# One-core hybrid encoder layer with mixture of experts: single-pass gather, third-largest expert at 64 rows, two more modulation blocks on VectorE, splits 3 to 1 by GpSimd

## The chip, the cores and the metric

The kernel runs on one core of a Trainium2 chip. The metric is device time in microseconds for one execution, the median of the runs of a kernel. Its engines are TensorE (PE, with the weight load shown apart as PEld), VectorE (DVE, `V` in the code), ScalarE (ACT, `S`), GpSimd (POOL, `G`) and SyncE (SP, whose queue issues nearly all transfers). The work of each engine runs in the order in which the program lists it.

## The reference

One encoder layer on 256 positions of width 2048, in fp32. `c` gives six modulation rows of 2048 each (shift, scale and gate of the mixer, sections 0 to 2; the same of the expert part, sections 3 to 5):

```python
c_act = silu(c)
mod = c_act @ w_ada + b_ada                  # 2048 x 12288
sh1, sc1, g1, sh2, sc2, g2 = split(mod, 6)
h = rms_norm(x, g_mix) * (1 + sc1) + sh1
z = h @ w_in                                 # 2048 x 4616
y = concat[gmlp(z), pool(z), forgetting_attention(z)]
x = x + g1 * (y @ w_out)
h = rms_norm(x, g_ffn) * (1 + sc2) + sh2
scores = sigmoid(h @ w_router)               # 16 experts, 4 groups
# best group of each position, its best 2 experts, weights normalised
x = x + g2 * sum over the 2 experts of weight * (silu(h @ w_gate[e]) * (h @ w_up[e])) @ w_down[e]
```

The 16 experts have matrices 2048 x 1024, 2048 x 1024 and 1024 x 2048. Each of the 256 positions goes to two of them, so 512 assignments are spread over the experts.

## The kernel before

**Dense part.** Weights come through ring tiles of 1 MiB (`ring`, `spare`, later `ringm`), issued on SP's queue. A product that must be accurate is made of three fp32r products (`mm3`): `split` writes the high part of a 128x512 weight tile by a ScalarE cast and the low part by a subtraction on VectorE or GpSimd, as a letter of `WSPLIT` (w_in) or `WSO` (w_out) says. Four letters stand for the four 128-row tiles of one piece (512 x 512 weights). `step` runs the preparation of tiles four ahead of their products. w_in is gone through in five chunks of rows (`CHUNKS`, 2, 2, 4, 4 and 4 tiles of 128); for each, `make_h` brings the normalised, modulated columns of x into the form `hT`, and nine pieces are multiplied and added into `z` (`put`). `PLAN` and `LAST` list by hand what goes between the pieces of a chunk: modulation steps (`n`, `m`, `0`, `1`), attention steps (`a`), norms (`w`).

A modulation block (512 columns of a section) is `c_act @ w_ada` for four ring tiles. `ada_parts` makes it on TensorE, as 16 products with a one-column operand into four rows of a PSUM bank (32 rows in the trace, two for each); `sum_parts` makes it on VectorE, as 16 multiply-adds over 128x512 (L292, L294), the last of which leaves PSUM (`ga`). The letters of `M1A`, `M1B`, `M2A`, `M2B` and `G1` say which. Both kinds use the two banks `accs`. The gate rows (sections 2 and 5) get their bias by one more product with `bgt`.

w_out is four column blocks of four pieces. A block's two PSUM banks are multiplied by the gate and added to x by `x1_block`; the banks come from a pool of three (`pm`).

**Handover.** The router's logits come from x (`logit_a`, `logit_b`). Then one long VectorE chain picks groups and experts (`oh1`, `oh2`, `M`), counts (TensorE products into `pp`), orders the experts by their count (`key`, `ohc`, `po`), and writes the expert numbers to `irow`, which SP reads to know which weights to load. It goes on to the slot of each assignment and to one-hot matrices `oneh` (128 x 512 for each half of x). The remaining gate blocks of section 5 run on TensorE in between (`g2_run`). `gather` multiplies x (fp32) by `oneh`: 512 slots of tokens, sorted by expert, in `XT`. Slots 0 to 255 are gathered before the banks are handed over, slots 256 to 511 after it; `oneh` lies in the last ring tile.

**Expert part.** Experts are taken by rank of their count; `CAPS` gives each rank its number of rows (128, 64 or 32), `ORDER` the order of the ranks, and the last rank is left out. An expert is twelve tiles of 2 MiB in six ring tiles (`wide`): eight for gate and up, four for down. At 128 rows the weights are split in the same way and multiplied three times (`el`); at 64 and 32 rows the fp32 weights are used. If a rank has more tokens than rows, a loop at the end takes that expert once more (`n_ov`).

## Time and profile before

| | |
|---|---|
| median of 3 runs | 1436.28 us (1435.34 to 1439.57) |
| the profiled execution | 1442.07 us, its span 1440.2 us |
| mean granted TensorE clock | 0.962 |
| busy: TensorE, VectorE, ScalarE, GpSimd | 87%, 48%, 29%, 11% of the span |
| moved | 539 MB, 374 GB/s over the span |

The span is what lies between the first and the last instruction of the profiled execution; times in the rows count from its start. Weights alone are 535.85 MB read. The dense part ends at about 476 us with the router's logits, the expert part begins at 532 us.

### The profile page before, as it was taken

Reading aid. Unit: us, or ns where it says so; the run is one execution under the profiler, and the core shown is the slowest. Engines: PE = TensorE matmul, PEld = TensorE weight load, DVE = VectorE, ACT = ScalarE, POOL = GpSimd, SP = SyncE. Lnnn points to the kernel's source line nnn. Section 1 sums busy time; section 2 is a strip of 40 time slices with the busy share of each in tenths; the row PEclk is TensorE's granted clock in tenths of the full one; section 3 lists DMA queues with packets and bytes.
Section 4 is the critical chain, followed back from the end, with each engine's and each line's share of the span. In section 5 each row is a group of like instructions: output and inputs, shape, how many; then the busy total and the mean of one; then the engine's idle time right before and its main releaser. Section 6 shows DMA issues by size and latency. Waiting matters only on the chain.

```text
span 1440.2 us, 17629 instructions
## 1 busy us (share of the span) xinstructions
PE 1247.2 (87%) x6844; PEld 683.4 (47%) x6844; DVE 693.2 (48%) x1271; ACT 417.1 (29%) x754; POOL 160.5 (11%) x127
## 2 busy tenths in 40 slices
PE   5998999998999896999969999689997889858876
PEld 3665776664776372764326743257533222222221
DVE  4466675755795643893228842269611211202112
ACT  4532334445343140771006820048300000000000
POOL 1333332312443000000000000000000000000000
PEclk9999999999999898999989999899999999989988
DMA  9979696889888579998999989999899999999997
GB/s 391 377 312 348 237 375 227 313 334 352 355 301 344 212 296 428 427 415 339 427 426 426 424 315 428 428 425 427 308 420 426 425 427 427 426 427 426 427 427 296
DMA packets 49209, 539.15 MB, mean 374 GB/s; under 512 B 5464, under 2 KB 5592, under 8 KB 7008
## 3 DMA queue, kind: packets, MB, share of 16 engines
q1 hardware_dynamic: 47664, 534.79, 90.7%
q10 hardware_dynamic: 1456, 3.17, 0.6%
q8 instruction: 55, 0.90, 0.3%
q14 instruction: 34, 0.28, 0.1%
HBM read 535.85 MB, written 2.10 MB: 374 GB/s over the span
## 4 chain that ended last, share of the span: by engine, by line
PE 59%; DMA 26%; DVE 7%; issue 3%; ACT 2%; POOL 1%; SPq 0%; DVEq 0%; ACTq 0%; POOLq 0%
PE lbank L171 29%; PE pm L171 18%; DMA ring<-in_e_down_dram 11%; DMA ringl<-in_e_gu_dram 7%; DMA ring<-in_e_gu_dram 7%; PE bank L171 6%; PE ada L171 4%; PE pt L171 1%; DVE ada L294 1%; DMA ring<-in_w_ada_dram 1%; DVE whl L176 1%; DVE el L176 1%; ACT whl L175 1%; DVE z L451 1%; POOL whl L176 0%
## 5 line engine op out<-in xcount | busy, mean ns | idle before, releaser
L171 PE MATMUL pm<-whl,hT 128*128 128x512 f32 x1120 | 296.6, 400 | 9.7 <-DVE whl L176 3.9
L171 PEld LDWEIGHTS pm<-whl,hT 128*128 128x128 f32 x1120 | 208.8, 190 | 82.9 <-issue 12.8
L171 PE MATMUL lbank<-ringl,xr 128*32 128x256 f32 (+1 forms) x1152 | 143.1, 494 | 38.1 <-DMA ringl<-in_e_gu_dram 37.8
L171 PE MATMUL lbank<-el,xs 128*128 128x512 f32 x576 | 138.3, 398 | 9.5 <-ACT el L175 6.5
L176 POOL TENSOR_TENSOR whl<-ring,whl 128x512 fp32r<-128x512 f32 x86 | 120.0, 1407 | 225.4 <-ACT whl L175 201.9
L171 PE MATMUL lbank<-ring,xr 128*32 128x256 f32 (+1 forms) x864 | 104.3, 484 | 34.8 <-DMA ring<-in_e_gu_dram 34.7
L171 PEld LDWEIGHTS lbank<-el,xs 128*128 128x128 f32 x576 | 108.1, 190 | 39.9 <-ACT el L175 9.7
L175 ACT CAST whl<-ring 128x512 fp32r<-128x512 f32 x172 | 99.9, 622 | 72.6 <-PE pm L171 62.5
L171 PE MATMUL bank<-y,gt 128*128 128x512 f32 x240 | 118.0, 614 | 0.0
L1304 DVE TENSOR_TENSOR xa<-xa,bank 128x512 f32<-128x512 f32 x120 | 82.5, 688 | 68.5 <-PE bank L171 68.5
L171 PE MATMUL lbank<-ring,hidT 128*64 128x512 f32 (+1 forms) x576 | 104.6, 630 | 10.9 <-DMA ring<-in_e_down_dram 10.9
L171 PEld LDWEIGHTS lbank<-ringl,xr 128*32 128x32 f32 (+1 forms) x1152 | 52.0, 127 | 129.1 <-issue 68.0
L1295 DVE TENSOR_TENSOR y<-lbank,g2w 128x512 f32<-128x512 f32 x60 | 41.5, 692 | 147.9 <-PE lbank L171 147.9
L176 DVE TENSOR_TENSOR whl<-ring,whl 128x512 fp32r<-128x512 f32 x86 | 83.9, 991 | 38.0 <-ACT whl L175 37.7
L175 ACT CAST el<-ring 128x512 fp32r<-128x512 f32 x144 | 90.0, 625 | 29.3 <-PE lbank L171 21.6
L176 DVE TENSOR_TENSOR el<-ring,el 128x512 fp32r<-128x512 f32 x144 | 92.7, 689 | 0.0
L1191 ACT COPY gt<-bank 128x256 f32<-128x256 f32 x15 | 5.6, 373 | 290.0 <-PE bank L1189 290.0
L1245 DVE TENSOR_TENSOR hid<-hid,lbank 128x512 f32<-128x512 f32 x12 | 8.3, 688 | 164.7 <-PE lbank L171 164.5
L171 PEld LDWEIGHTS lbank<-ring,xr 128*32 128x32 f32 (+1 forms) x864 | 39.1, 127 | 98.8 <-DMA ring<-in_e_gu_dram 48.9
L171 PE MATMUL ada<-ring,cact 128*1 128x512 f32 (+1 forms) x568 | 68.6, 585 | 19.7 <-DMA ring<-in_w_ada_dram 14.0
L171 PE MATMUL lbank<-el,hidT 128*128 128x512 f32 x288 | 74.9, 412 | 12.1 <-DVE el L176 8.3
L175 ACT CAST el<-ringl 128x512 fp32r<-128x512 f32 x96 | 58.7, 624 | 79.5 <-DMA ringl<-in_e_gu_dram 64.8
(377 smaller groups left out, 1185.4 us busy)
## 6 DMA issues: line engine op xcount, KB each, us to landing
ringl<-in_e_gu_dram SPq DMA_DIRECT2D x60, 2048.0 KB, 20.1
ring<-in_e_gu_dram SPq DMA_DIRECT2D x45, 2048.0 KB, 24.3
ring<-in_e_down_dram SPq DMA_DIRECT2D x45, 2048.0 KB, 25.7
ring<-in_w_ada_dram SPq DMA_DIRECT2D x79, 1024.0 KB, 7.1
ring<-in_w_in_dram SPq DMA_DIRECT2D x30, 1024.0 KB, 8.2
ringm<-in_e_gu_dram SPq DMA_DIRECT2D x15, 2048.0 KB, 21.0
ringm<-in_e_down_dram SPq DMA_DIRECT2D x15, 2048.0 KB, 21.5
ring<-in_w_out_dram SPq DMA_DIRECT2D x12, 1024.0 KB, 8.2
```

Source lines behind the costliest of these rows:

```text
L171: E.matmul(out, lhsT=lhsT, rhs=rhs, start=start, stop=stop, skip_group_check=True)
L175: S.copy(hi, src)
L176: (eng or V).tensor_tensor(lo, src, hi.bitcast(F32), op=OP.subtract)
L294: eng.scalar_tensor_tensor(P, w[:, j, :], ck, P, op0=OP.mult, op1=OP.add)
L451: V.tensor_tensor(dst, dst, P[h], op=OP.add)
L1191: S.copy(gt, p[:, :256])
L1245: V.tensor_tensor(hid[:, o], hid[:, o], P[2 * b + 1], op=OP.mult)
L1295: V.tensor_tensor(y, P, g2w[:, c0:c0 + 512], op=OP.mult)
L1304: V.tensor_tensor(a, a, p, op=OP.add)
```

## The change

- `CAPS`: the third rank has 64 rows instead of 128.
- `M2A` "VVPP": the first two blocks of section 3 move from TensorE to VectorE, so seven modulation blocks are there. `WSPLIT` and `WSO`: in the last three chunks and in w_out three of four tiles are split by GpSimd.
- `make_h`: x is scaled by ScalarE (`scaled`) and transposed, instead of multiplied by a diagonal matrix.
- The three `pm` banks are fixed tiles; from w_out on the second modulation bank joins them as the fourth, and all gate blocks use the first one.
- Gate biases: eight row transfers on ScalarE's queue (`bgr`) and an add on VectorE (`gate_row`, L797), instead of a product with `bgt`.
- The gather uses x in two fp32r parts (`x_hi` on ScalarE, `x_lo` on VectorE, L1004) for all 512 slots at once, before the banks are handed over. The operands lie where the last two ring tiles (`ringl`) lie afterwards; the older ring tiles are loaded first.

```diff
-CAPS = [128] * 3 + [64] * 6 + [32] * 6 + [0]
+CAPS = [128] * 2 + [64] * 7 + [32] * 6 + [0]
-M1A, M1B, M2A, M2B, G1 = "PPVV", "PPPP", "PPPP", "PPPP", "PVVV"
-WSPLIT, WSO = ["VGVG"] * 5, "VGVG"
+M1A, M1B, M2A, M2B, G1 = "PPVV", "PPPP", "VVPP", "PPPP", "PVVV"
+WSPLIT, WSO = ["VGVG", "VGVG", "GVGG", "GVGG", "GVGG"], "GVGG"
...
-    psM, s_psM = pool("psM", 3, space=PSUM)
+    psM, s_psM = pool("psM", 1, space=PSUM)
+    pbanks = deque(psM.tile([128, 512], F32, name=f"pm{i}") for i in range(3))
+
     def pm():
-        return psM.tile([128, 512], F32, name="pm")
+        pbanks.rotate(-1)
+        return pbanks[-1]
...
-                if g == ng - 1 and bias is not None:
-                    mm(P[0:1, :], ident[0:8, bias:bias + 1], bgt, start=False)
...
+    def scaled(q):
+        k0, nk = CHUNKS[q]
+        for h in range(2):
+            S.activation(xn[:, h, :128 * nk], xa[:, h, 128 * k0:128 * k0 + 128 * nk], AF.Identity, scale=rsx[:, h:h + 1])
...
-                mm(p[:, 128 * h:128 * h + 128], xa[:, h, 128 * k:128 * k + 128], diag[:, h, :])
+                E.transpose(p[:, 128 * h:128 * h + 128], xn[:, h, 128 * c:128 * c + 128], ident)
...
+    def gate_row(sec, q, out, P):
+        S.copy(out, P)
+        o = slice(32 * q, 32 * q + 1)
+        V.tensor_tensor(out[o, :], out[o, :], bgr[o, sec // 3, :], op=OP.add)
+
     def gate_args(sec, q, out):
-        return sec, 4 * q, 4, lambda P: S.copy(out, P), q % 2, 4 * (sec // 3) + q
+        return sec, 4 * q, 4, lambda P: gate_row(sec, q, out, P), 0
...
+    bgr = rt.tile([128, 2, 512], F32, name="bgr")
+    for q in range(4):
+        for a in range(2):
+            nc.scalar.dma_start(bgr[32 * q:32 * q + 1, a, :], bg_d[a:a + 1, 512 * q:512 * q + 512])
...
+    g1_load(1)
+    pbanks.append(accs[1])
...
+    def x_hi():
+        for c, h in parts:
+            o = slice(1024 * c, 1024 * c + 1024)
+            S.activation(xhl[:, 0, h, o], xa[:, h, o], AF.Identity, scale=rs1[:, h:h + 1])
+
+    def x_lo(n):
+        for _ in range(n):
+            c, h = parts.pop(0)
+            o = slice(1024 * c, 1024 * c + 1024)
+            V.scalar_tensor_tensor(xhl[:, 1, h, o], xa[:, h, o], rs1[:, h:h + 1], xhl[:, 0, h, o].bitcast(F32),
+                                   op0=OP.mult, op1=OP.subtract)
...
     V.reciprocal(sc, sc)
+    x_hi()
...
+    x_lo(2)
...
     V.tensor_copy(irow[:, 0:16], po[0:1, 0:16])
+    x_lo(2)
...
-    def gather(half, k, bank):
-        o = slice(256 * half, 256 * half + 256)
-        p = bank()
+    def gather(k):
+        p = pm()
         for h in range(2):
-            mm(p[:, :256], xa[:, h, 128 * k:128 * k + 128], oneh[:, h, o], start=h == 0, stop=h == 1)
+            for i in range(2):
+                mm(p, xhl[:, i, h, 128 * k:128 * k + 128], oneh[:, h, :], h + i == 0, h + i == 2)
...
+    s_phl.close()
+    pl, s_pl = pool("pl", 1, side="right")
+    wides += [pl.tile([128, 2 * RINGW], F32, name=f"ringl{i}") for i in range(RING_LAST)]
+    wide_ring = deque([t for _, t in sorted(zip(used, old), key=lambda x: x[0])] + wides[RING + RING_MORE:])
...
-    for k in range(KD):
-        gather(1, k, bank)
```

Where instructions come to stand. First VectorE's queue in the handover, from `M` (both experts of each position) to `irow` (the expert numbers); `grow` are the gate rows, `xhl` the two parts of x. Before:

```order
L1001 TENSOR_TENSOR M<-oh_3680,oh_3687 128x32
L1029 SCALAR_TENSOR_TENSOR key<-pt_119,rev 128x16
L1030 SCALAR_TENSOR_TENSOR keyc<-pt_119,revc 16x1
L1032 TENSOR_SCALAR rkc<-key,keyc 16x16
L1033 TENSOR_REDUCE rkc<-rkc 16x1
L1035 TENSOR_SCALAR ohc<-ioE,rkc 16x16
L1041 CAST irow<-pt_120 1x16
```

Now:

```order
L1050 TENSOR_TENSOR M<-oh_3602,oh_3609 128x32
L797 TENSOR_TENSOR grow_3322<-grow_3322,bgr 1x512
L797 TENSOR_TENSOR grow_3323<-grow_3323,bgr 1x512
L1004 SCALAR_TENSOR_TENSOR xhl<-xa,rs_3524,xhl 128x1024 x2
L1079 SCALAR_TENSOR_TENSOR key<-pt_122,rev 128x16
L1080 SCALAR_TENSOR_TENSOR keyc<-pt_122,revc 16x1
L1082 TENSOR_SCALAR rkc<-key,keyc 16x16
L1083 TENSOR_REDUCE rkc<-rkc 16x1
L1085 TENSOR_SCALAR ohc<-ioE,rkc 16x16
L797 TENSOR_TENSOR grow_3324<-grow_3324,bgr 1x512
L1091 CAST irow<-pt_123 1x16
```

Two bias adds and two low parts have come ahead of `key`, and the bias add of the last gate block ahead of `irow`.

Next SP's queue from the last gate tiles to the loads of the first expert (`ring_63`, `ring_64`, `ring_65`, `ringm` are the older ring tiles, `ringl` the last two). Before:

```order
L147 DMA ring_64<-in_w_ada_dram 128x2048
L1316 TENSOR_LOAD irow
L1312 ISA
L1312 DMA ringl_3792<-in_e_gu_dram 128x4096
L1312 ISA
L1312 DMA ringl_3793<-in_e_gu_dram 128x4096
L1312 ISA
L1312 DMA ringm_2773<-in_e_gu_dram 128x4096
```

Now:

```order
L147 DMA ring_64<-in_w_ada_dram 128x2048
L1356 TENSOR_LOAD irow
L1352 ISA
L1352 DMA ringm_2671<-in_e_gu_dram 128x4096
L1352 ISA
L1352 DMA ring_65<-in_e_gu_dram 128x4096
L1352 ISA
L1352 DMA ring_63<-in_e_gu_dram 128x4096
```

The four older tiles come first, the two `ringl` tiles behind them.

Last VectorE's queue in the last chunk, from the norm factors of the first heads (`hr`) on; `z<-z,hr` are the norms, `z<-z,pm` the puts, `ada` the sums of a modulation block, `whl` the splits. Before:

```order
L352 TENSOR_TENSOR hr_1893<-hr_1893,hr1t 128x16
L176 TENSOR_TENSOR whl<-ring_64,whl 128x512
L451 TENSOR_TENSOR z<-z,pm 128x512 x2
L176 TENSOR_TENSOR whl<-ring_64,whl 128x512
L569 TENSOR_TENSOR z<-z,hr_1893 128x512 x2
L451 TENSOR_TENSOR z<-z,pm 128x512 x2
L176 TENSOR_TENSOR whl<-ring_63,whl 128x512
L584 TENSOR_SCALAR qk<-pt_120,prm_69 128x256
L558 TENSOR_REDUCE ss_2008<-pt_119 128x4
L558 TENSOR_REDUCE ss_2008<-ada_113 128x4
L176 TENSOR_TENSOR whl<-ring_63,whl 128x512
```

Now:

```order
L292 TENSOR_SCALAR ada_114<-ring_63,cact 128x512
L294 SCALAR_TENSOR_TENSOR ada_114<-ring_63,cact,ada_114 128x512 x3
L573 TENSOR_TENSOR z<-z,hr_1825 128x512 x2
L454 TENSOR_TENSOR z<-z,pm_119 128x512
L454 TENSOR_TENSOR z<-z,pm_120 128x512
L294 SCALAR_TENSOR_TENSOR ada_114<-ring_64,cact,ada_114 128x512 x4
L588 TENSOR_SCALAR qk<-pt_123,prm_69 128x256
L562 TENSOR_REDUCE ss_1936<-pt_122 128x4
L562 TENSOR_REDUCE ss_1936<-ada_113 128x4
L294 SCALAR_TENSOR_TENSOR ada_114<-ring_65,cact,ada_114 128x512 x4
L176 TENSOR_TENSOR whl<-ring_63,whl 128x512
```

Three times four multiply-adds have come in, and two of the splits have gone.

## Rows read from the trace of the kernel before

**Rows 1.** The page, part 2: the span in 40 slices of 36 us, GB/s moved in each.

```profile
GB/s 391 377 312 348 237 375 227 313 334 352 355 301 344 212 296 428 427 415 339 427 426 426 424 315 428 428 425 427 308 420 426 425 427 427 426 427 426 427 427 296
```

**Rows 2.** Two stretches of the dense part: start and end, length, then busy time (instructions) of PE, PEld, DVE, ACT and POOL, granted clock, share of the transfer engines, GB/s. The first is the last chunk of w_in, the second w_out.

```profile
226.00:358.00 132.00, 125.67 (x750) 79.17 (x749) 82.11 (x194) 63.66 (x141) 31.39 (x27) 1.00 0.83 312
358.00:471.00 113.00, 106.13 (x509) 78.97 (x508) 81.95 (x103) 44.64 (x85) 48.05 (x38) 0.97 0.86 334
```

**Rows 3.** The same columns for stretches of the handover and of the expert part.

```profile
488.00:496.00 8.00, 6.97 (x52) 2.53 (x50) 4.70 (x20) 0.59 (x1) 0.00 (x0) 1.00 0.00 0
496.00:520.00 24.00, 21.85 (x84) 16.70 (x83) 18.60 (x61) 12.35 (x22) 0.00 (x0) 0.93 0.95 389
520.00:532.00 12.00, 12.00 (x55) 9.10 (x53) 3.81 (x7) 3.62 (x7) 0.00 (x0) 1.00 0.23 98
...
646.00:676.00 30.00, 29.08 (x120) 13.69 (x120) 12.83 (x22) 6.37 (x11) 0.00 (x0) 1.00 0.82 310
676.00:826.00 150.00, 129.38 (x733) 71.23 (x730) 79.82 (x133) 53.06 (x89) 0.00 (x0) 0.94 1.01 426
826.00:868.00 42.00, 40.16 (x165) 19.30 (x165) 18.03 (x30) 9.79 (x17) 0.00 (x0) 1.00 0.86 329
868.00:1006.00 138.00, 118.28 (x679) 64.07 (x674) 72.94 (x122) 46.86 (x79) 0.00 (x0) 0.94 1.01 427
1006.00:1054.00 48.00, 45.23 (x185) 24.18 (x185) 24.91 (x41) 16.08 (x27) 0.00 (x0) 1.00 0.86 331
1054.00:1420.00 366.00, 287.34 (x1746) 97.69 (x1742) 65.47 (x123) 5.79 (x13) 0.00 (x0) 0.95 1.01 427
```

**Rows 4.** The page, part 5: the matmuls of the three experts with 128 rows, gate and up first, then down (count; busy us, mean ns; idle before).

```profile
L171 PE MATMUL lbank<-el,xs 128*128 128x512 f32 x576 | 138.3, 398 | 9.5 <-ACT el L175 6.5
...
L171 PE MATMUL lbank<-el,hidT 128*128 128x512 f32 x288 | 74.9, 412 | 12.1 <-DVE el L176 8.3
```

**Rows 5.** The waits of SP's queue from 486 to 500 us (total us, times, longest).

```profile
SPq L1316 <- DVE pos L1045: 11.2, 1, 11.2
SPq L1312 <- PE ada L171: 3.6, 1, 3.6
```

**Rows 6.** The timeline of SP's queue: start, us, issue, count.

```profile
496.39 0.89 SPq L1312 DMA_DIRECT2D ringl<-in_e_gu_dram  x2
...
532.22 0.33 SPq L1312 DMA_DIRECT2D ring<-in_e_gu_dram  x1
```

**Rows 7.** The chain that ended last, the piece of the second half of the gather: start, us, engine, name, line, count.

```profile
517.89 14.31 PE bank L171 x64
```

**Rows 8.** Groups of instructions from 0 to 480 us, shapes apart: TensorE's modulation blocks, VectorE's sums, GpSimd's splits, and two ScalarE operations over 512 and 2048 columns.

```profile
L176 POOL TENSOR_TENSOR whl<-ring,whl 128x512 fp32r<-128x512 f32 x86 | 120.0, 1407 | 225.4 <-ACT whl L175 201.9 <-PE ada L171 15.5 <-issue 8.0
L175 ACT CAST whl<-ring 128x512 fp32r<-128x512 f32 x172 | 99.9, 622 | 72.6 <-PE pm L171 62.5 <-DMA ring<-in_w_in_dram 4.2 <-DVE z L451 2.7
...
L171 PE MATMUL ada<-ring,cact 128*1 128x512 f32 x408 | 51.7, 596 | 5.6 <-DVE ga L297 4.4 <-ACT r L311 1.2
...
L294 DVE SCALAR_TENSOR_TENSOR ada<-ring,cact,ada 128x512 f32<-128x512 f32 x54 | 40.7, 754 | 1.5
...
L375 ACT ACTIVATE hT<-xa 128x2048 fp32r<-128x2048 f32 x2 | 3.8, 1902 | 0.3 <-DMA xa<-in_x_dram 0.3
```

**Rows 9.** The split's line L176: duration in ns, shortest/median/longest, first and last start, shape.

```profile
L176 DVE TENSOR_TENSOR whl<-ring,whl x86: 677/693/1803, 25.4 to 450.2; 128x512 fp32r<-128x512 f32 x86
L176 POOL TENSOR_TENSOR whl<-ring,whl x86: 1257/1296/1798, 26.0 to 451.7; 128x512 fp32r<-128x512 f32 x86
```

**Rows 10.** The timeline of the dense part: start, us, engine, line, out<-in, count, in brackets the idle time before and what ended it.

```profile
127.04 1.04 PE L171 MATMUL ada<-ring,cact 128*1 128x512 f32 x8 [4.41 <-DVE ga L297]
...
253.28 1.38 DVE L451 TENSOR_TENSOR z<-z,pm 128x512 f32<-128x512 f32 x2
...
267.20 5.78 PE L171 MATMUL pm<-whl,hT 128*128 128x512 f32 x24
```

**Rows 11.** TensorE's waits from 360 to 476 us (total us, times, longest).

```profile
PE pm L171 <- DVE xg L855: 3.7, 3, 1.8
```

**Rows 12.** The timeline of the handover: the Exp of the scores, the gate blocks of TensorE (`ada`), VectorE's `key`, `irow` and first one-hot (it lies in `ring`).

```profile
478.76 0.23 ACT L969 ACTIVATE sc<-sc 128x32 f32<-128x32 f32 x1 [2.25 <-DVE sc L968]
482.35 3.59 PE L171 MATMUL ada<-ring,cact 128*1 128x512 f32 x16
485.71 2.21 PE L171 MATMUL ada<-ringm,cact 128*1 128x512 f32 x16
490.40 0.17 DVE L1029 SCALAR_TENSOR_TENSOR key<-pt,rev 128x16 f32<-128x16 f32 x1 [5.61 <-PE pt L171]
491.71 3.61 PE L171 MATMUL ada<-ring,cact 128*1 128x512 f32 x32
491.82 0.16 DVE L1041 CAST irow<-pt 1x16 int32<-1x16 f32 x1 [0.48 <-PE pt L171]
495.70 0.54 DVE L1085 TENSOR_SCALAR ring<-io,sl,rs 128x512 f32<-128x512 f32 x1
```

**Rows 13.** Three stretches of the handover, columns as in rows 2; the granted clock is the third number from the end.

```profile
480.00:486.00 6.00, 6.00 (x26) 0.78 (x26) 4.08 (x24) 0.59 (x1) 0.00 (x0) 0.50 0.88 330
...
500.00:504.00 4.00, 4.00 (x13) 3.21 (x12) 3.66 (x15) 1.56 (x3) 0.00 (x0) 0.57 1.01 428
504.00:532.00 28.00, 28.00 (x121) 21.50 (x119) 14.89 (x46) 13.69 (x24) 0.00 (x0) 1.00 0.68 287
```

More of the change, by code (lines that the diff above doesn't have):

```diff
@@ L253, in ada_load, with ada_parts @@
         return w.rearrange("p (k n) -> p k n", n=n)
-    def ada_parts(sec, k0, nk, after, acc, bias=None):
+    def ada_parts(sec, k0, nk, after, acc):
         P = accs[acc]
@@ L266, in run @@
                     k, t = r * g + j, j % 4
-                    mm(P[32 * t:32 * t + 1, :128 * nk], cact[:, k:k + 1], w[:, j, :], start=k < 4,
-                       stop=k >= KD - 4 and (t > 0 or bias is None))
-                if g == ng - 1 and bias is not None:
-                    mm(P[0:1, :], ident[0:8, bias:bias + 1], bgt, start=False)
+                    mm(P[32 * t:32 * t + 1, :128 * nk], cact[:, k:k + 1], w[:, j, :], start=k < 4, stop=k >= KD - 4)
                 if g == ng - 1:
@@ L377, in body @@
     rsqrt(rsx, ssx, D, [128, 2], "rx")
-    diag = pa.tile([128, 2, 128], F32, name="diag")
-    for h in range(2):
-        V.tensor_scalar(diag[:, h, :], ident, rsx[:, h:h + 1], None, op0=OP.mult)
     jc = pa.tile([128, 16], F32, name="jc")
@@ L516, in body @@
         f()
+    scaled(0)
     flush()
@@ L692, in body @@
     g1_first = []
-    mod2.extend((f, None) for f in steps(ada_parts(2, 0, 4, lambda P: g1_first.append(P), 1, 0)))
+    mod2.extend((f, None) for f in steps(ada_parts(2, 0, 4, lambda P: g1_first.append(P), 1)))
     for i in range(4, 33, 4):
@@ L720, in body @@
                 piece(q, PIECES[i])
+            if i == 1:
+                then(lambda q=q: scaled(q + 1))
             for c in PLAN[q][i]:
@@ L904, in g1_steps @@
         if n == 0:
-            S.copy(r4s[0], g1_first[0])
+            gate_row(2, 0, r4s[0], g1_first[0])
             return []
@@ L908, in g1_steps @@
             return steps(ada_parts(*gate_args(2, n, r4s[n])))
-        return steps(sum_parts(2, 4 * n, 4, lambda a: None, n % 2, ENG(G1[n]), lambda: r4s[n], n))
+        return steps(sum_parts(2, 4 * n, 4, lambda a: None, 0, ENG(G1[n]), lambda: r4s[n], n))
     r4s = []
@@ L931, in body @@
             ws[g]()
-            g1_load(1)
+            if n + g:
+                g1_load(1)
             if n == 3 and g == 0:
@@ L957, in body @@
     logit_b(3)
+    s_py.close()
+    s_hp.close()
+    s_pb.close()
+    s_c1.close()
+    pg2, s_pg2 = pool("pg2", 1, side="right")
+    g2w = pg2.tile([128, D], F32, name="g2w")
+    XT = pg2.tile([128, KD, 512], F32, name="XT")
+    phl, s_phl = pool("phl", 1, side="right")
+    xhl = phl.tile([128, 2, 2, D], F32R, name="xhl")
+    oneh = phl.tile([128, 2, 512], F32R, name="oneh")
+    parts = [(c, h) for c in range(2) for h in range(2)]
+    def x_hi():
[8 more added lines that the diff above has]
+                                   op0=OP.mult, op1=OP.subtract)
     B3 = [128, 2, 16]
@@ L1055, in body @@
     pick(start, tmp, cnt)
-    s_py.close()
-    s_hp.close()
-    s_pb.close()
-    s_c1.close()
-    pg2, s_pg2 = pool("pg2", 1, side="right")
-    g2w = pg2.tile([128, D], F32, name="g2w")
-    wides += [pg2.tile([128, 2 * RINGW], F32, name=f"ringl{i}") for i in range(RING_LAST)]
-    old = wides[:RING + RING_MORE]
-    used = [max(i for i, x in enumerate(ring_tiles) if x is a or x is b) for a, b in halves_of]
-    wide_ring = deque(wides[RING + RING_MORE:] + [t for _, t in sorted(zip(used, old), key=lambda x: x[0])])
-    def wide():
-        wide_ring.rotate(-1)
-        return wide_ring[-1]
-    XT = pg2.tile([128, KD, 512], F32, name="XT")
-    oneh = wide_ring[-1][:, :1024].rearrange("p (h s) -> p h s", h=2)
     sl1 = rtile(B3, "sl1")
@@ L1105, in body @@
     for k in range(KD):
-        gather(0, k, pm)
+        gather(k)
     cntR = rtile([128, 16], "cntR")
@@ L1161, in body, with wide @@
         S.copy(g2w[:, 512 * b:512 * b + 512], p)
+    s_phl.close()
+    pl, s_pl = pool("pl", 1, side="right")
+    wides += [pl.tile([128, 2 * RINGW], F32, name=f"ringl{i}") for i in range(RING_LAST)]
+    old = wides[:RING + RING_MORE]
+    used = [max(i for i, x in enumerate(ring_tiles) if x is a or x is b) for a, b in halves_of]
+    wide_ring = deque([t for _, t in sorted(zip(used, old), key=lambda x: x[0])] + wides[RING + RING_MORE:])
+    def wide():
+        wide_ring.rotate(-1)
+        return wide_ring[-1]
     s_rt.close()
@@ L1378, in body @@
         down_stage(128, hid, gt, load, store)()
-    for s in (s_pg2, s_ring2, s_ring, s_cst, root):
+    for s in (s_pl, s_pg2, s_ring2, s_ring, s_cst, root):
         s.close()
```

27 lines of the change are left out of this document (14 added, 13 removed).

## Prediction

> **What bounds the kernel now.** I read the page first, then the kernel cut into stretches, then the queue's waits, and last the timeline of the stretch in which one stage hands over to the next. The page's GB/s line shows two kernels in one [rows 1]: in its first 15 slices (to 540 us) the rate swings between 212 and 391; from the 16th on it stands at 415 or more, but for three dips (339, 315, 308) and the last slice. The stretches say what limits each part. In the dense part TensorE is busy for 125.7 of 132 us and 106.1 of 113 us while the transfers run at 312 and 334 GB/s [rows 2]: TensorE is the bound, in program order. In the expert part the transfers are: 366 us at 427 GB/s from 1054 us on, whatever the engines do [rows 3]. A 2 MiB tile takes 2.097/0.427 = 4.91 us there, and fifteen experts have twelve each: 884 us that can't shrink. A change in the expert part is worth only what it returns of lost transfer time.
>
> Lost transfer time stands in five places. Three dips of 310, 329 and 331 GB/s come with the three experts of 128 rows [rows 3]; their matmuls alone take 138.3 + 74.9 us for three, 71 each [rows 4], against 12 x 4.91 = 59 us of loading, so the six ring tiles fill and the queue waits. Between and behind them, where experts of 64 and 32 rows run, stand 426 and 427 GB/s [rows 3]. The other two places are the handover: nothing moves from 488 to 496 us, and 98 GB/s from 520 to 532 [rows 3]. SP waits 11.2 us for the expert numbers, then 3.6 us for TensorE [rows 5], issues five tiles from 496.39 on, and the sixth at 532.22 [rows 6]: that tile holds `oneh` until the second half of the gather, 14.3 us of TensorE, is through [rows 7].
>
> **The change part by part.** The sum is made against the profiled execution, 1442.07 us, 0.4% above the median of 1436.28.
>
> *Third expert with 64 rows.* Lost at the third dip: 48 us x (427 - 331)/427 = 10.8 us. The first two lost 30 x 117/427 = 8.2 and 42 x 98/427 = 9.6, and stay. Behind the third dip the transfers run full to the end, so what is returned there reaches the end. Bounds 8 and 13; I take **-10.8**. It needs at most 64 tokens on the third expert. Evaluating the reference's routing on its inputs gives 77, 70, 62, 59, 56, 33 and fewer: it fits, by two.
>
> *Two more modulation blocks on VectorE* (`M2A`). On TensorE 408 rows cost 51.7 us, so a block's 32 rows 4.05 [rows 8]; two blocks are 8.1 us less. VectorE pays 16 x 0.754 = 12.1 us a block [rows 8]. The first block is spread over two chunks, two steps of 3.0 us in each, and nine splits a chunk leave VectorE (9 x 0.69 = 6.2 us [rows 9]): covered, -4. The second falls where VectorE is full. From 253.28 [rows 10] its queue would hold put 1.4, sum 3.0, norms 3.0, put 1.4, sum 3.0, `qk` and squares 1.9, sum 3.0, split 0.7: done at 270.7. TensorE came to that piece at 267.20 [rows 10]; three steps of 1 us earlier now, and with one tile (1.4 us) in hand, it stands from 265.6 to 270.7. That is 5 us against 4 saved: +1. That sums on VectorE can hold TensorE up, the trace shows: 4.41 us at 127 us [rows 10]. Together **-3**, bounds -8 and +5.
>
> *Splits 3 to 1 by GpSimd.* Three take 3 x 1.407 = 4.2 us [rows 8] in the time of 24 matmuls, 5.78 us [rows 10]: GpSimd stays below the pace. Cost nothing; the cover is 1.6 us in four tiles, and without it every piece is longer by what is missing. A lone split takes 0.693 us on VectorE and 1.296 on GpSimd, the longest 1.803 and 1.798 [rows 9]. The Trainium skill (SBUF — State Buffer, Who interferes with whom) says that a VectorE instruction with two SBUF inputs and a GpSimd one that reads SBUF shut each other out. By it four tiles would cost 3 x 1.296 + 0.693 = 4.6 us of the shared port, still less than TensorE's time; with the longest rows alone 3 x 1.798 = 5.4, just less. So it makes a pacing GpSimd unlikely, but not absurd. The sums keep their running total in PSUM, one SBUF input, and no row shows them slowed: the trace agrees.
>
> *Fourth bank for w_out.* TensorE waits 3.7 us, three times in all, until VectorE has read a bank between column blocks [rows 11]; ScalarE's and GpSimd's queues may keep a part: **-3** (0 to -5). *Bias rows:* eight small transfers now stand on ScalarE's queue ahead of the first w_out casts; at SP's 0.33 us an issue [rows 6] 2.6 us, mostly under a wait for VectorE's first split that is there already: **+1** (0 to +3). *Scaled transposes* replace as many matmuls of the same size; the scaling is ScalarE's, a piece ahead, while it waits for TensorE: nothing, at worst 1 us a chunk. Front: **-5**, bounds -14 and +6.
>
> *The handover.* VectorE's bias adds (L797) and the low parts of x (L1004) now stand in its queue ahead of `key` and of `irow`, and all gate blocks share one PSUM bank. Step by step, on the old clock: ScalarE ends Exp at 479.0 [rows 12] and makes four high parts of 1024 columns, some 1.05 us each (between half of 1.902 and twice 0.622 [rows 8]), to 483.2; the copy of the gate block before it goes to 483.8, and TensorE's next block, now on the same bank, starts at 484.0 instead of 482.35 [rows 12]. That block took 5.6 us, mostly at half clock [rows 12, 13]: 489.6. Its copy and VectorE's add end at 491.2, two low parts (0.69 to 1.39 us each by the splits, I take 1.3) at 493.9, where `key` stood at 490.40. TensorE's last block came 1.3 us after `key` began [rows 12]: 495.2, after an idle stretch of 4 us. It takes 3.6 us at full clock [rows 12], 5.6 if it begins at half; the half level has stood behind such gaps twice (0.50 from 480, 0.57 from 500) [rows 13], so 500.8. The Trainium skill (TensorE: Matmul & The Clock Gate) has half clock after idling too, and the trace agrees. Copy and add: `irow` at 502.6, where it was at 491.82. SP had read the number by 496.39 - 3.6 = 492.8 [rows 5, 6], 0.8 us after that cast: the first tile goes at 503.6, not at 496.39. VectorE goes on with two low parts (2.6) and the 3.9 us that lie between `irow` and the first one-hot [rows 12], then 2.4 for both pairs: the gather begins at 510.8. It is 64 matmuls of 512 columns at 5.78/24 = 0.24 us, 15.4, and 1.5 more for half clock at its start: its end is 527.7. Four tiles are in by 503.6 + 1.7 + 19.6 = 525 (1.7 is what the stretch from 496 to 520 lost, 24 x 38/427, less 0.4 before the issue [rows 3]). The two new ring tiles lie where the gather's operands lay and are issued at 528. The stream that went on at 532.2 with five tiles done goes on at 528 with four done: 4.2 - 4.9. So **+1**, bounds -6 (full clock, short low parts) and +15 (half clock throughout). The 14.3 us of the second half are gone, but a later routing chain eats them.
>
> **Sum.** -10.8 - 5 + 1 = -15: 1427 on the profiled execution, 1421 on the median.
>
> **Rivals.**
> - *The handover pays.* If TensorE keeps full clock and the low parts take 0.7 us, `irow` is at about 500 and the gather over by 521; then the four tiles count, in by 522: 6 us better than above, and a dense part nearer its lower bound gives another 5: 1410. For it speaks the full clock from 488 to 496 [rows 3]; against it the idle stretches of 4 and 10 us that the order makes.
> - *The dense part gives nothing:* stalls behind VectorE's sums take all that TensorE saves. Then the dip remains, 1436.28 - 10 = 1426. The 4.41 us stall speaks for it, the splits that leave VectorE against it.
> - *The gather comes late:* at half clock throughout it takes 31 us and the stream goes on 14 us later: 1435, no change. Against it: from 504 on, after such a gap, the old gather ran at full level [rows 13].
> - *Slower, GpSimd paces the dense part.* The 43 pieces that are split 3 to 1 then lose what three splits take over TensorE's 5.78 us. It turns the result when a piece loses over 15/43 = 0.35 us, at splits of 2.04 us; at 2.15 us the kernel is at 1450. The longest row, 1.798, is below that.
> - *Slower, overflow:* a third expert with 65 tokens or more sends one whole expert, 59 us of loading at least, through the loop behind everything else: 1480 or more. The count of 62 speaks against it.
>
> **Chances.** My forecast 0.50 (own range 1414 to 1428), the handover pays 0.15, the dense part gives nothing 0.20, the late gather 0.09, GpSimd 0.04, overflow 0.02. The range for 8 in 10 takes in the rivals next to the forecast: 1407 to 1432. What a measurement of this kernel can tell from no change is about 0.3%, 4.3 us: faster 0.85, within 0.09, slower 0.06.
>
> **What would show it.** Right: two dips in GB/s instead of three, and 427 from the second on; `irow` 6 to 11 us later than now, counted from the last logits; no second half of the gather, and no stretch of 12 us without transfers ahead of the sixth tile; TensorE standing still at the fifth piece of the last chunk. Wrong: a third dip behind some expert of 64 rows (then the ring, not the rows, made the dips), a last bias add that doesn't hold `irow`, waits of TensorE for GpSimd's splits of over 10 us in the dense part.

## The result, and the profile after

| | before | changed |
|---|---|---|
| median (four runs each) | 1437.77 us | 1429.01 us (1425.25 to 1430.1) |
| the profiled execution | 1442.07 us, span 1440.2 | 1425.25 us, span 1423.5 |

The ratio is 0.9931, with a 95% interval from 0.9915 to 0.9946: 9.9 us faster (7.8 to 12.2), where 15 were forecast; the two medians alone lie 8.8 apart. The predicted time was 1421, the range 1407 to 1432.

The page's GB/s line of the changed kernel, 40 slices of 35.6 us, against [rows 1]:

```profile
GB/s 390 383 321 347 215 381 232 270 357 354 339 315 375 183 350 428 426 421 320 427 426 427 426 334 426 426 426 428 426 427 427 426 427 427 427 427 427 426 427 302
```

Two dips are left (320 and 334), and from the second on every full slice stands at 426 to 428. The weakest slice is the 14th in both, at 183 now and at 212 before.

The same columns as in [rows 2, 3], for the handover and the expert part of the changed kernel:

```profile
485.00:498.00 13.00, 7.51 (x56) 2.76 (x48) 5.37 (x11) 1.17 (x2) 0.00 (x0) 0.87 0.07 28
498.00:518.00 20.00, 12.99 (x45) 10.14 (x46) 18.59 (x59) 7.80 (x10) 0.00 (x0) 0.74 0.95 390
518.00:523.00 5.00, 5.00 (x23) 3.98 (x22) 4.16 (x14) 4.28 (x6) 0.00 (x0) 1.00 0.29 125
...
856.00:1385.00 529.00, 428.69 (x2438) 143.69 (x2434) 95.97 (x180) 8.09 (x18) 0.00 (x0) 0.94 1.01 427
```

Next to nothing moves from 485 to 498 us (before: from 488 to 496), then four tiles come, and the 12 us at 98 GB/s ahead of the sixth tile have become 5 us at 125. The timeline of the handover says why, beside [rows 12]; ACT copies a gate block to `grow`, DVE adds its bias (L797), makes low parts (L1004), `key`, `irow` and the one-hots, PE runs the gate blocks (`ada<-ring`) and the gather (`xhl`):

```profile
473.22 1.03 PE L171 MATMUL lgp<-x1T,wra 128*16 128x256 f32 x8
477.13 4.25 ACT L998 ACTIVATE xhl<-xa,rs 128x1024 fp32r<-128x1024 f32 x4
481.90 1.90 PE L171 MATMUL ada<-ring,cact 128*1 128x512 f32 x16 [1.84 <-ACT grow L795]
486.90 2.48 DVE L1004 SCALAR_TENSOR_TENSOR xhl<-xa,rs,xhl 128x1024 fp32r<-128x1024 f32 x2
489.30 0.17 DVE L1079 SCALAR_TENSOR_TENSOR key<-pt,rev 128x16 f32<-128x16 f32 x1
490.81 4.96 PE L171 MATMUL ada<-ring,cact 128*1 128x512 f32 x32
496.47 0.69 DVE L797 TENSOR_TENSOR grow<-grow,bgr 1x512 f32<-1x512 f32 x1 [6.25 <-ACT grow L795]
497.19 0.16 DVE L1091 CAST irow<-pt 1x16 int32<-1x16 f32 x1
505.00 5.73 PE L171 MATMUL pm<-oneh,xhl 128*128 128x512 f32 x12 [9.23 <-DVE oneh L1118]
521.52 1.07 PE L171 MATMUL ada<-oneh,xhl 128*128 128x512 f32 x4
```

and SP's queue, which issues the first tile 1.0 us behind `irow` and the last two ring tiles (`ringl`) when the gather ends:

```profile
498.17 0.35 SPq L1352 DMA_DIRECT2D ringm<-in_e_gu_dram  x1
498.80 1.51 SPq L1352 DMA_DIRECT2D ring<-in_e_gu_dram  x3
522.71 0.87 SPq L1352 DMA_DIRECT2D ringl<-in_e_gu_dram  x2
```

VectorE had the order of the experts (`ohc`) at 490.2 and waited 6.25 us for a gate block whose bias stands in its queue ahead of `irow`. The order of the queue is now what holds the stream.

### The profile page after: what moved, and what is told of

Read it like the earlier page. It is cut to its first block, busy times and chain, and to the rows that moved or that the text cites. A ratio compares the mean times of both kernels' runs of the same rounds, so it can differ in the third digit from the quotient of the medians.

```text
span 1423.5 us, 16962 instructions
## 1 busy us (share of the span) xinstructions
PE 1204.0 (85%) x6582; PEld 631.1 (44%) x6582; DVE 613.4 (43%) x1155; ACT 363.6 (26%) x659; POOL 215.2 (15%) x170
## 4 chain that ended last, share of the span: by engine, by line
PE 53%; DMA 34%; DVE 5%; issue 3%; ACT 2%; POOL 1%; SPq 0%; ACTq 0%; DVEq 0%; POOLq 0%
PE lbank L171 23%; PE pm L171 18%; DMA ring<-in_e_down_dram 13%; DMA ring<-in_e_gu_dram 9%; DMA ringm<-in_e_gu_dram 8%; PE ada L171 5%; PE bank L171 4%; DMA ringl<-in_e_down_dram 2%; DMA ringl<-in_e_gu_dram 2%; PE pt L171 1%; POOL whl L176 1%; DMA ring<-in_w_ada_dram 1%; DVE ada L294 1%; DVE z L454 1%; DVE el L176 0%
## 5 line engine op out<-in xcount | busy, mean ns | idle before, releaser
L176 POOL TENSOR_TENSOR whl<-ring,whl 128x512 fp32r<-128x512 f32 x121 | 164.4, 1376 | 194.1 <-ACT whl L175 189.3
L171 PE MATMUL lbank<-ring,xr 128*32 128x256 f32 (+1 forms) x1216 | 156.1, 497 | 33.4 <-DMA ring<-in_e_gu_dram 33.4
L175 ACT CAST whl<-ring 128x512 fp32r<-128x512 f32 x172 | 99.8, 621 | 72.7 <-PE pm L171 53.6
L171 PE MATMUL lbank<-ringl,xr 128*32 128x256 f32 (+1 forms) x608 | 81.3, 520 | 32.0 <-DMA ringl<-in_e_gu_dram 32.0
L171 PE MATMUL lbank<-ringm,xr 128*32 128x256 f32 (+1 forms) x608 | 81.6, 511 | 25.9 <-DMA ringm<-in_e_gu_dram 25.2
L171 PE MATMUL lbank<-el,xs 128*128 128x512 f32 x384 | 91.1, 395 | 6.5 <-ACT el L175 4.6
L171 PEld LDWEIGHTS lbank<-el,xs 128*128 128x128 f32 x384 | 71.3, 188 | 26.4 <-ACT el L175 6.8
L171 PE MATMUL lbank<-ringl,hidT 128*64 128x512 f32 (+1 forms) x416 | 74.2, 598 | 3.2 <-DMA ringl<-in_e_down_dram 3.2
L454 DVE TENSOR_TENSOR z<-z,pm 128x512 f32<-128x512 f32 x72 | 48.5, 685 | 60.2 <-PE pm L171 60.1
L171 PEld LDWEIGHTS bank<-y,gt 128*128 128x128 f32 x240 | 41.8, 192 | 72.9 <-issue 70.5
L176 DVE TENSOR_TENSOR whl<-ring,whl 128x512 fp32r<-128x512 f32 x51 | 50.9, 1001 | 45.0 <-ACT whl L175 44.9
```

Of the source, the lines that this page charges most:

```text
L171: E.matmul(out, lhsT=lhsT, rhs=rhs, start=start, stop=stop, skip_group_check=True)
L175: S.copy(hi, src)
L176: (eng or V).tensor_tensor(lo, src, hi.bitcast(F32), op=OP.subtract)
L454: V.tensor_tensor(dst, dst, P[h], op=OP.add)
```

## The experiments

Single executions scatter by several us, so each trace is cut at four marks that the same rows give in every kernel: the first add into `z` (L451, now L454, in e11 L452), the start of the last eight products of the logits (`lgp`), the issue with which the stream goes on (the sixth tile before, the first `ringl` tile in the changed kernel), the end of the span. Behind the third mark the changed kernels have one tile more to load than the old one, 4.9 us; the last column but one leaves it out. The dips are summed from stretches of 10 us, 10 x (427 - rate)/427 each.

| kernel | first put | to last logits | to restart | to the end, less the tile | dips, us lost |
|---|---|---|---|---|---|
| before | 60.8 | 414.2 | 57.2 | 908.0 | 8.4, 9.3, 10.3 |
| before again (e12) | 59.7 | 414.2 | 53.9 | 903.8 | 8.4, 9.3, 7.8 |
| before, 64 rows (e5) | 60.4 | 415.8 | 52.3 | 899.0 | 9.3, 9.7 |
| changed | 60.3 | 412.9 | 49.5 | 895.9 | 9.3, 7.8 |
| 128 rows again (e1) | 62.4 | 411.0 | 51.1 | 906.5 | 8.1, 8.4, 10.6 |
| blocks on TensorE (e2) | 60.5 | 407.9 | 50.8 | 895.5 | 8.3, 8.3 |
| splits even (e3) | 63.9 | 417.5 | 51.4 | 899.9 | 10.0, 10.0 |
| adds late (e4) | 63.6 | 411.0 | 37.7 | 895.7 | 7.7, 8.0 |
| adds late, again (e7) | 60.8 | 411.0 | 37.7 | 899.2 | 9.2, 7.5 |
| three banks (e6) | 63.6 | 412.4 | 49.6 | 897.9 | 7.9, 8.3 |
| blocks on TensorE, splits even (e8) | 63.4 | 408.1 | 53.6 | 899.6 | 9.3, 10.8 |
| adds late, blocks on TensorE (e9) | 62.1 | 407.9 | 37.5 | 895.7 | 7.7, 8.0 |
| adds late, one block (e10) | 61.9 | 411.7 | 37.8 | 898.4 | 9.2, 9.7 |
| diagonal (e11) | 60.5 | 412.4 | 51.2 | 896.1 | 9.0, 7.6 |

Times in us below are differences of ratios times 1438.

**The third expert.** e1 undoes it in the changed kernel, e5 makes it alone in the kernel before.

```diff
-CAPS = [128] * 2 + [64] * 7 + [32] * 6 + [0]
+CAPS = [128] * 3 + [64] * 6 + [32] * 6 + [0]
```

> The changed kernel with one edit undone: the third expert has 128 rows again. Theory (the dip behind a 128-row expert is what its matmuls take beyond its loads, and comes back whole): 11 to 12 us longer than the changed kernel, about 1.001 to 1.002 of the kernel before, and a third dip near 330 GB/s where the third expert stands. Rival (the six ring tiles, whichever expert runs, make the dips, and they only move): within 4 us of the changed kernel, 0.991 to 0.996 of the kernel before.

> The kernel before with one edit: the third expert has 64 rows. Theory (the third dip alone is worth what the trace of before shows lost there): 10 to 11 us shorter than the kernel before, 0.992 to 0.993, two dips in GB/s instead of three, and everything up to the second expert as before. Rival (the dip's price depends on what stands around it; the changed kernel with the edit undone was only 8.3 us longer): 6 to 9 us, 0.994 to 0.996. Its trace also shows the old handover in another execution: if the block of gate rows that ran at half clock in the trace of before does not do so here, the sixth tile is issued less than 57 us after the last logits.

Measured: e1 0.9989 (0.9973 to 1.0004), 8.3 us above the changed kernel; e5 0.9941 (0.9927 to 0.9955), 8.5 us below the kernel before. The page's GB/s lines, e1 first, in fences of their own:

```profile
GB/s 391 359 334 331 226 379 230 268 355 348 358 328 372 155 371 428 426 406 346 429 426 427 427 325 429 427 426 427 309 417 426 427 427 426 428 427 427 426 427 298
```

```profile
GB/s 390 382 319 339 244 352 228 313 338 353 359 285 359 231 312 428 427 421 319 428 426 427 427 310 427 428 425 427 426 428 425 427 428 427 427 426 427 427 427 290
```

The dip goes and comes with the rows (309 in the 29th slice of e1, 426 there in e5), so the rival that the ring makes it falls. Both theories asked too much: e1 misses its 11 to 12, and e5 lies in the band of its rival, by which the price depends on what stands around the dip; but it is much the same in both kernels. It is 8.4, not 10.8: the dips of all fourteen traces lie between 7.5 and 10.8, and the forecast had taken one at the upper end.

**The two modulation blocks and the splits.** e2 puts the blocks back on TensorE (the first line of the edit), e3 the splits back to two and two (the second line), e8 both.

```diff
-M1A, M1B, M2A, M2B, G1 = "PPVV", "PPPP", "VVPP", "PPPP", "PVVV"
-WSPLIT, WSO = ["VGVG", "VGVG", "GVGG", "GVGG", "GVGG"], "GVGG"
+M1A, M1B, M2A, M2B, G1 = "PPVV", "PPPP", "PPPP", "PPPP", "PVVV"
+WSPLIT, WSO = ["VGVG"] * 5, "VGVG"
```

> The changed kernel with the two blocks of section 3 back on TensorE. Theory A, from the two traces (the last puts of the chunks stand 1.0 us earlier, 0.15 later and 2.9 later than before, although TensorE has 8.1 us less to do): the sums on VectorE hold TensorE up by more than they save, so this is about 4 us shorter than the changed kernel, 0.989 to 0.991 of the kernel before, and the stall of 4.3 us for qk in the last chunk is gone. Rival B, the step of the prediction (the blocks save 3 us together): 3 us longer, 0.995 to 0.996. Rival C (the stalls come from the splits on GpSimd, not from the sums): 4 to 8 us longer, with the stalls still there.

> The changed kernel with the splits two to two by VectorE and GpSimd, the two blocks still on VectorE. Theory A (VectorE is full where the blocks are summed, and nine splits more in a chunk, 6.2 us, come on top): longer by 5 to 12 us, 0.996 to 1.002 of the kernel before, with longer waits of TensorE for VectorE in the last three chunks. Rival B (GpSimd with three splits of four sets the pace): shorter by 2 us or more, 0.992 or less. Rival C (neither is full): within 2 us.

> The changed kernel with the two blocks back on TensorE and the splits two to two, so that VectorE and GpSimd have the dense work that they had before. Theory (the splits to GpSimd are worth something only where VectorE is full, which it is with the blocks): within 2 us of the kernel with the blocks alone undone, 0.989 to 0.992 of the kernel before. Rival (VectorE is full in the last chunk with or without the blocks): 3 to 6 us longer than that, 0.992 to 0.995.

Measured: e2 0.9902 (0.9888 to 0.9916), e3 0.998 (0.9963 to 0.9996), e8 0.9933 (0.9915 to 0.9952). TensorE's waits from 60 to 360 us (total us, times, longest) of the changed kernel, then of e2, then of e3:

```profile
PE pm L171 <- DVE whl L176: 5.2, 2, 2.6
PE pt L324 <- DVE qk L588: 4.3, 1, 4.3
PE ada L171 <- DVE ga L297: 3.8, 1, 3.8
PE pm L171 <- POOL whl L176: 1.5, 3, 0.7
```

```profile
PE ada L171 <- DVE ga L297: 3.8, 1, 3.8
PE pm L171 <- DVE whl L176: 2.2, 1, 2.2
PE pm L171 <- POOL whl L176: 0.7, 1, 0.7
```

```profile
PE ada L171 <- DVE ga L297: 5.7, 1, 5.7
PE pt L324 <- DVE qk L588: 4.9, 1, 4.9
PE pm L171 <- DVE whl L176: 4.0, 6, 1.1
```

With the blocks on TensorE the wait for `qk` is gone and that for VectorE's splits falls from 5.2 to 2.2 us. By the marks the dense part is 3.1 us shorter (407.9 against the 411.0 of e1, e4 and e7, which share it with the changed kernel), by the time the kernel is 4.2 shorter: the blocks cost. Up to the last put it is even 4.6 shorter (268.7 against 273.3). The rest is lost again at the first product of w_out, which waits for ScalarE's cast, in the changed kernel and in e2:

```profile
363.17 0.50 PE L171 MATMUL pm<-whl,hT 128*128 128x512 f32 x1 [3.19 <-ACT whl L175]
```

```profile
360.14 0.65 PE L171 MATMUL pm<-whl,hT 128*128 128x512 f32 x1 [4.96 <-ACT whl L175]
```

Ahead of that cast ScalarE's queue issues the eight bias rows: 2.36 us in the changed kernel, while the transfers stand nearly still (4 GB/s), and 4.13 in e2, which gets there earlier, while they run at 280 GB/s. GpSimd never holds TensorE for more than 0.7 us at a time, so rival C of e2 and rival B of e3 fall. Undoing the splits costs 6.5 us by the marks (417.5) and 7.0 by the time as long as the blocks are on VectorE; without the blocks it costs 0.3 by the marks (408.1 against 407.9). The time of e8 is 4.5 longer than e2's, in the band of its rival, but its trace spends that elsewhere: 2.9 ahead of the first put, 2.8 between logits and restart, 3.5 in the dips. For the dense part the theory of e8 holds; what its whole time says is not settled.

**The handover.** e4 changes only VectorE's order.

```diff
     def gate_row(sec, q, out, P):
         S.copy(out, P)
-        V.tensor_tensor(out[o, :], out[o, :], bgr[o, sec // 3, :], op=OP.add)
+        late_add.append(lambda: V.tensor_tensor(out[o, :], out[o, :], bgr[o, sec // 3, :], op=OP.add))
+        if sec == 2:
+            late_add.pop()()
...
-    x_lo(2)
+    x_lo(4)
     SQ = [128, 16, 16]
...
     V.tensor_copy(irow[:, 0:16], po[0:1, 0:16])
-    x_lo(2)
...
     V.tensor_copy(irow[:, 32:48], stc[0:1, :])
+    for f in late_add:
+        f()
```

> The changed kernel with VectorE's queue in the handover in another order: the bias adds of section 5 stand behind the one-hots, and all four low parts of x ahead of key, so that nothing slow stands between key, the expert numbers and the one-hots. Theory (the bias add behind the last gate block holds the chain, 6.2 us of idle VectorE, and the stream waits for the gather's end): the expert numbers 5 to 7 us earlier counted from the last logits, the gather 7 to 9 us earlier, the last two ring tiles with it, so 6 to 9 us shorter than the changed kernel, 0.987 to 0.989 of the kernel before. Rival (the stream is held by the four first tiles, which are not loaded sooner, or TensorE runs the gather at half clock): 0 to 3 us shorter, 0.991 to 0.993.

> One more look at the kernel with the adds behind the one-hots, for the spread of its parts between two executions: first put to last put of the dense part 273 to 274 us, last logits to the issue of the last two ring tiles 37 to 39 us.

(The second, e7, is the same kernel once more.) Measured: e4 0.9836 (0.9819 to 0.9852), 13.7 us faster than the changed kernel, 23.6 faster than the one before. Its timeline:

```profile
474.59 1.03 PE L171 MATMUL lgp<-x1T,wra 128*16 128x256 f32 x8
484.29 4.87 DVE L1008 SCALAR_TENSOR_TENSOR xhl<-xa,rs,xhl 128x1024 fp32r<-128x1024 f32 x4
491.28 3.61 PE L171 MATMUL ada<-ring,cact 128*1 128x512 f32 x32
491.39 0.16 DVE L1095 CAST irow<-pt 1x16 int32<-1x16 f32 x1 [0.48 <-PE pt L171]
492.37 0.35 SPq L1357 DMA_DIRECT2D ringm<-in_e_gu_dram  x1
496.69 0.70 PE L171 MATMUL pm<-oneh,xhl 128*128 128x512 f32 x2 [1.79 <-DVE oneh L1121]
498.84 2.82 DVE L797 TENSOR_TENSOR grow<-grow,bgr 1x512 f32<-1x512 f32 x4
512.25 0.87 SPq L1357 DMA_DIRECT2D ringl<-in_e_gu_dram  x2
```

From the last logits to `irow` 16.8 us instead of 24.0, to the gather 22.1 instead of 31.8, to the restart 37.7 instead of 49.5. The bias adds are still done in time: they run under the gather. The rival of the four first tiles falls. It is more than the 6 to 9 expected mainly because the gather itself is shorter, 15.4 us (496.69 to the last products, which end at 512.13) instead of 17.6: TensorE had idled 9.2 us ahead of it in the changed kernel and began at half clock, and only 1.8 us here. The restart comes at 37.5 to 37.8 us in all four traces with this order.

**Together, and one block alone.** e9 is e4 with M2A "PPPP", e10 e4 with "VPPP".

> Both undone steps together: the adds behind the one-hots and all low parts ahead of key, and the two blocks back on TensorE. Theory (the two lie in different stretches and add up): 0.980 to 0.982 of the kernel before, some 1409 to 1412 us; first put to last put 268.5 to 269.5 us, last logits to the issue of the last two ring tiles 37 to 39. Rival (what the dense part ends earlier is lost again, as the last gate tiles or the clock come later): 0.983 to 0.984, like the adds alone.

> The kernel with the adds behind the one-hots, and only the first of the two blocks on VectorE, which is spread over the third and fourth chunk. Theory A, the step of the prediction (the first block is covered and saves 4 us, the second costs): 4 us or more shorter than with two blocks, as short as or shorter than with none: 0.979 to 0.981. Theory B, from the traces (the third chunk gains 1.1 us by the block, the fourth loses 2.7, the last loses 3.5 by the second block): first put to last put 270 to 270.6 us, 0.981 to 0.983.

Measured: e9 0.9844 (0.9827 to 0.9861), e10 0.9844 (0.9822 to 0.9866). The marks of e9 are as its theory says (407.9 and 37.5, and its profiled execution is the shortest of all, 1409.83 us), but the time misses the 0.980 to 0.982 and lies just above the rival's band: the median is 1414.73 against 1414.93 of e4, and the 3 us of the dense part do not show in it. e2 had shown 4.2 us. The intervals of e4 and e9 overlap, so whether the blocks are worth moving back once the handover is mended stays open. For e10 theory A falls: with the first block alone the dense part is 411.7, no shorter than with both, though the last chunk's stall is gone. Theory B misses its marks too (271.9 us from first put to last put), but its chunks hold: the fourth takes 64.1 us, as with both blocks, and the last 105.7, where e4 has 108.4 and e2 105.4. What the last chunk gains is lost elsewhere: 1.3 us in the first two chunks (granted clock 0.86 from 93 to 105 us, where e4 has 1.00 from 95 to 107), and 2.1 behind the last put, 1.6 of it the wait at w_out's first product (4.8 us, with 3.96 for the issue of the bias rows).

**Bank and transposes.** e6 leaves out `pbanks.append(accs[1])`; e11 brings the product with the diagonal matrix back into `make_h` and leaves out `scaled`.

> The changed kernel with three banks in w_out and in the gather, the second modulation bank no longer joined to them. Theory (between column blocks TensorE waits for VectorE's reading, 3.7 us in all): 3 to 4 us longer than the changed kernel, 0.995 to 0.996 of the kernel before, the three waits of 0.2, 1.8 and 1.8 us back at the first product of the later column blocks. Rival (GpSimd with three splits of four, or the loads, take what the bank gives): within 1.5 us of the changed kernel.

> The changed kernel with the scaled transposes undone: x is multiplied by a diagonal matrix again. Theory, the step of the prediction (as many TensorE instructions of the same size, the scaling hidden on ScalarE): within 2 us of the changed kernel, 0.992 to 0.994. Rival (the scaling stands in ScalarE's queue ahead of casts that the last chunks wait for): 2 to 4 us shorter, 0.990 to 0.992.

Measured: e6 0.995 (0.9936 to 0.9964), 2.7 us longer than the changed kernel, 1.4 by the marks. TensorE's wait for VectorE's reading in e6, where [rows 11] has 3.7 us in three waits:

```profile
PE pm L171 <- DVE xg L874: 1.3, 2, 0.6
```

Two thirds of that wait are gone without the bank, presumably by the splits, which leave VectorE less to do ahead of it; no run has three banks and even splits. e6's interval overlaps that of the changed kernel, so its time alone does not decide between theory and rival. e11 0.9932 (0.9913 to 0.9951): no change, as its theory says. Its dense part is 1.4 longer than that of e1, e4 and e7, and its first put, 60.5, is among the earliest of the changed kernels (60.3 to 63.9; more of that below).

> One more look at the kernel before, unchanged, for the spread of its parts. Theory (in the trace of before a block of gate rows ran at half clock, in that of the same kernel with 64 rows for the third expert it did not, and the handover was 5 us shorter): last logits to the issue of the sixth tile either near 52 or near 57 us, and the time of the execution with it; first put to last put 270 to 272 us.

The kernel before, once more: 1433.44 us, 8.6 below its first trace, with the same order and nearly the same dense part. In [rows 13] the second gate block ran at a granted clock of 0.50; here it did not. The rows of the block's two halves, where [rows 12] has 3.59 and 2.21 us, and of SP's queue:

```profile
479.88 1.90 PE L171 MATMUL ada<-ring,cact 128*1 128x512 f32 x16
481.60 1.90 PE L171 MATMUL ada<-ringm,cact 128*1 128x512 f32 x16
...
487.39 0.16 DVE L1041 CAST irow<-pt 1x16 int32<-1x16 f32 x1 [0.48 <-PE pt L171]
...
493.65 34.47 SPq L1312 DMA_DIRECT2D ring<-in_e_gu_dram  x3
```

The logits stand at 473.86 there: 13.5 us to `irow`, where the first trace has 16.8. Its restart is at 493.65 + 34.47 - 0.33 = 527.79.

## Why the prediction was right, and where it was not

The direction and the largest term's mechanism were right, the size two thirds: 9.9 us of the 15. The marks give an account by parts, each from a few single executions. Means over the traces that share a part: expert part 906.1 (three traces with three dips) against 897.5 (eleven with two), -8.6; handover 54.5 - 4.9 = 49.6 (before, e5, e12) against 51.0 (the seven with the changed one), +1.4; dense part 414.7 against 411.5 (the changed kernel, e1, e4 and e7, which share it), -3.3; first put +1.9 (60.3 in before, e5, e12 against 62.2 in the ten with scaled transposes; the last section has what is known of it). Together -8.6, within the measured 7.8 to 12.2. No run undoes the bias rows or the gather alone; their parts are argued from the rows. That the dense part's -3.3 lies near the -5 of the front is luck: two errors in it cancel, as the next points show.

- *Third expert, -10.8: right mechanism, mis-sized; it measured -8.4.* The step read one dip of one execution. The same dip of the same kernel lost 7.8 in e12. The other two dips, 8.2 and 9.6 in the prediction's own text, were the hint that 10.8 was high.
- *Two blocks, -3: the wrong sign; they measure +3.1 by the marks.* The step that failed is "covered, -4" for the first block: against e2 the third chunk gains 1.1 by it and the fourth loses 2.7. The sum counted the splits that leave VectorE and not what stands in those chunks already: `M1A` "PPVV" sums a block on VectorE in the third and in the fourth chunk. Rows of the fourth in the changed kernel, VectorE's and TensorE's:

```profile
173.88 3.12 DVE L294 SCALAR_TENSOR_TENSOR ada<-spare,cact,ada 128x512 f32<-128x512 f32 x4
176.91 0.68 DVE L176 TENSOR_TENSOR whl<-ring,whl 128x512 fp32r<-128x512 f32 x1
177.51 0.75 DVE L292 TENSOR_SCALAR ada<-spare,cact 128x512 f32<-128x512 f32 x1
...
177.65 18.59 PE L171 MATMUL pm<-whl,hT 128*128 128x512 f32 x79 [2.60 <-DVE whl L176]
```

  A sum of the moved block, a split that TensorE waits for, and the first sum of the other block. From the third chunk's last put to its own the fourth chunk takes 64.1 us (161.03 to 225.17), and 61.5 in e2 (162.35 to 223.84). The second block's stall came as forecast: TensorE stands 4.3 us at the fifth piece where 5 were expected.

```profile
260.91 3.12 DVE L294 SCALAR_TENSOR_TENSOR ada<-ring,cact,ada 128x512 f32<-128x512 f32 x4
263.94 0.48 DVE L588 TENSOR_SCALAR qk<-pt,prm 128x256 f32<-128x256 f32 x1
...
264.47 0.76 PE L324 MATMUL pt<-ident,r 128*128 128x128 f32 x4 [4.30 <-DVE qk L588]
```

  Its price did not: the last chunk takes 108.8 us in the changed kernel and 108.4 in e4, against 105.4 in e2 and 105.7 in e10, so 3 us or more where +1 was forecast. The sum had the stall but not the clock behind it, 0.57 for 4 us (columns as in [rows 2]), where e2 has 1.00:

```profile
264.40:268.40 4.00, 3.93 (x16) 3.48 (x17) 3.89 (x7) 0.47 (x1) 0.00 (x0) 0.57 0.77 262
```

- *Splits, 0: right that GpSimd does not pace, wrong that they are worth nothing.* With the blocks on VectorE they are worth 6.5 us (e3). The prediction had spent them as cover for the blocks and still priced the pair at a gain; together they cost 2.9 by the marks, since e8, with neither, has a dense part of 408.1 against 411.0. In the time of e8, 0.9933 against 0.9931, that does not show.
- *Fourth bank, -3; bias rows, +1; transposes, 0.* The bank is worth 1.4 by the marks: two thirds of its wait were gone without it. The bias rows were priced by the queue that issues them alone; the products with `bgt` that they replace were forgotten. Two of them, of about 1 us each, stood in w_out or just ahead of it. w_out and what lies ahead of it, from the last put (331.08 before, 334.01 now) to the last logits, went from 143.9 to 139.2, and to 137.6 to 137.8 in four other traces with the same w_out (e1, e4, e7, e11); where w_out starts the granted clock is 0.62 in the changed kernel (362 to 370 us) and 0.79 in e4 (365 to 373). The transposes gave 1.4 in the dense part (e11), and nothing that the time shows.
- *Handover, +1: it measured +1.4*, less than its scatter (49.5 to 53.6 with the changed one), and its steps are the best part of the forecast. Counted in us from the last logits:

| step | forecast | trace |
|---|---|---|
| high parts of x ready | 8.2 | 8.2 |
| second gate block starts | 9.0 | 8.7 |
| it has run | 14.6 | 12.3 |
| `key` | 18.9 | 16.1 |
| last gate block starts | 20.2 | 17.6 |
| `irow` | 27.6 | 24.0 |
| first tile issued | 28.6 | 25.0 |
| gather begins | 35.8 | 31.8 |
| restart | 53.0 | 49.5 |

  One step differs by more than 1 us: the second block was taken at half clock, as in [rows 12, 13], and ran at full. What was gained by that is no gain against the old kernel, since its trace had paid for the half clock as well, and two further executions of the old handover (e5, e12) did not. The forecast took half clock from the gap ahead of the block, and the gap does not settle it: TensorE had waited 1.68 us ahead of the blocks that ran at half clock in the first trace, and 1.67 in e12, where they ran at full. One sum is off by 0.7: `irow` at 502.6 and the 2.6, 3.9 and 2.4 us behind it give 511.5 for the gather, not 510.8.
- *From trace to median.* The sum was made against one execution at 1442.07 and carried over to the median. That execution had a gate block at half clock (3 us to `irow`) and an expert part 4.2 us longer than e12's. What is removed from an execution that was unlucky there is too large; the pair of traces shows -16.7, the times -9.9.

Of the rivals, the one closest to what happened is that the dense part gives nothing: it gives 3.3 instead of 5. Stalls behind VectorE's sums do take what TensorE saves and more (blocks +3.1); w_out and the transposes bring the rest (-6). The late gather did not come, since half clock lasted 5 us of the gather and not all of it. "The handover pays" was within reach all the time: e4 has it at -12 against the kernel before (37.7 against 49.6), by the order of VectorE's queue alone.

## What to carry to other kernels

Work that is moved to an engine is priced by what that engine's queue holds at that very place, other moved work too: the average of the stretch said that VectorE had room, and the row ahead of the split that TensorE waited for said that it had not. In a serial chain that decides when a stream starts, nothing that waits for another engine may stand ahead of the chain's next step; here moving four adds of 0.7 us behind the one-hots, and the low parts of x into the wait ahead of `key`, was worth more than the whole change. A term read from a single dip or a single half-clock stretch wants a second execution, or the mean of its siblings in the same trace.
